# Index queries first, closings by column halves, and background work in finer steps, in a two-layer encoder on one core

## The chip, the core and the metric

The kernel runs as one program on one core of a Trainium2 chip. The engines have each their own instruction stream: PE multiplies matrices (and PEld loads its stationary operand), DVE and ACT do elementwise work, POOL a little of it, SP issues most transfers. The metric is the device time of one execution in microseconds (us).

## The reference

Two layers, each a mixer and a gated feed-forward network (FFN) with a convolution, on 512 positions of 1024 channels, in float32. Layer norm follows each of the two, with the residual scaled by ALPHA.

```python
for l in range(DEPTH):                                   # 2
    y = hybrid_mixer(x, positions, w_in[l], ..., w_out[l], b_out[l])
    x = layer_norm(DN_ALPHA * x + y, ln1_g[l], ln1_b[l])
    y = conv_ffn(x, w_up[l], conv_w[l], conv_b[l], w_down[l])
    x = layer_norm(DN_ALPHA * x + y, ln2_g[l], ln2_b[l])
...
# hybrid_mixer: proj = x @ w_in, split into aq, ak, av, iq, ik, iw, gq, gk, gv, g_lr, g_r, gate_a, gate_b
ya = dsa_attention(aq, ak, av, iq, ik, iw) @ p_attn      # iq.ik scores choose 128 keys a query; softmax over these
log_a = log_sigmoid(g_lr @ gla_w_gate + gla_b_gate) / 16
o = gla_chunked(gq, gk, gv, log_a)                       # state = exp(total) * state + k_dec^T v, by chunks of 64
yb = (norm(o) * silu(g_r)) @ p_gla
return (sigmoid(gate_a) * ya + sigmoid(gate_b) * yb) @ w_out + b_out
...
# conv_ffn: u = causal_conv3(x @ w_up) + conv_b; a, b = split(u); return (gelu(a) * b) @ w_down
```

## The kernel before

Every large product is made of three: each float32 operand is split into a rounded high part (ACT, line 144) and the rest (DVE, line 145), and `mm3` issues high x low, low x high and high x high (lines 149 to 151). A weight tile of 128 x 1024 (512 KB) is loaded by SP into one of three raw buffers (line 130) and split into one of five; `weight` keeps four tiles ahead, in the fixed order of `plan_all`. The split of a weight has priority in the schedule.

The input lies transposed in `xT` (8 tiles of 128 channels x 512 positions, high and low). `tm_chunk` makes a projection with positions in partitions: four quarters g of two weight rows each, and for every quarter the four position blocks tb; `fm_tile` makes one with channels in partitions. Sums are held in banks: `acc` has four, `tps` (transposes, and the state updates of the scans) and `sps` two each.

What isn't a projection runs as tasks. A task is a generator; `tick`, called every six products or so, lets each task issue its next step, up to its next `yield`. So the number of yields says how many products of the projections stand between two steps of a task. The tile framework then schedules all this into one fixed order for each engine.

Layer 0 begins with 14 warm-up products (line 905), the constants, the small projections (`do_small`: the index key, its weights and the decay's input, in a bank of `acc`), and the index queries "iq". During "gk", `decay_task` makes the decay logits (line 373), takes logarithms, splits them block by block and sums them by a triangular matrix (L390). `index_task` transposes the roped queries (L447, evacuated by `stack`), scores them (L476) and takes the largest 128 by rounds of max and match_replace (L509, L510). Two `scan_task`s, for two heads each, run beside the value, attention query and key projections: `update` (L536) makes both half-block contributions, DVE adds them to the state (L545, the first is copied, L542), the state is split, and `read` multiplies the queries with it.

`closing` is the last product of a mixer (`wout`) and of an FFN (`wdB`, eight of its 22 rows). It works by halves of the positions: two blocks x two column halves in four banks, and for both halves of the positions every weight row (128 x 1024) is loaded and split again. Its last three rows (five at the very end) are done sum by sum; DVE adds each sum to x (L837), and `norm` follows at once: statistics (L716, L718), an inverse root (`rstd`, a POOL operation L292 within, and L291 to L296 on DVE), two passes over x (L722, L723), and the transposes of x (L729) into `xT`, with their splits.

Of the kernel before, what the change touches and what calls it, by code (L numbers as in the profile page):

```python
# [23 lines left out]
RANK = 16  # L24
# [31 lines left out]
class Trunk:  # L56
# [86 lines left out]
    def split(self, hi, lo, src):  # L143
        self.nc.scalar.copy(hi, src)  # L144
        self.nc.vector.tensor_sub(lo, src, hi.bitcast(F32))  # L145

# [18 lines left out]
    def tm_chunk(self, l, chunk, evac, pairs=((0, 1, 2, 3),), between=None):  # L165
        ws = []
        for pair in pairs:
# [3 lines left out]
            for g in range(4):  # L171
                if len(ws) <= g:
                    ws.append(self.weight((l, chunk, g)))
                w = ws[g].rearrange("p z (k n) -> p z k n", k=2)
                for j, tb in enumerate(pair):
                    for kk in range(2):
                        k = 2 * g + kk
                        c = slice(tb * 128, (tb + 1) * 128)
                        self.mm3(ps[j], self.xT[:, k, 0, c], self.xT[:, k, 1, c], w[:, 0, kk], w[:, 1, kk],
                                 k == 0, k == KT - 1)  # L180
# [13 lines left out]
    def constants(self):  # L194
# [21 lines left out]
        self.xT = c.tile([128, KT, 2, S], F32R, name="xT")  # L216

    def rope_tables(self):
# [3 lines left out]
        nc.scalar.dma_start(pi_, self.a["positions"])  # L222
# [43 lines left out]
    def layer_consts(self, l):  # L266
# [3 lines left out]
        for r in (0, 32, 64):  # L270
            nc.scalar.dma_start(raw[r:r + RANK + 1, :], a["w_gate"][l])
# [4 lines left out]
        nc.scalar.dma_start(self.normg, a["norm_g"][l])  # L276
        self.convw = self.lay.tile([128, 2 * NF, 3], F32, name=self.name("cw"), tag="cw")
        nc.scalar.dma_start(self.convw, a["conv_w"][l])
        self.convb = self.lay.tile([128, 2 * NF], F32, name=self.name("cb"), tag="cb")
        nc.scalar.dma_start(self.convb, a["conv_b"][l])  # L280
# [19 lines left out]
    def plan_all(self, l):  # L300
# [38 lines left out]
        for half in range(2):  # L339
            for k in range(KA, NF):  # L340
                P((l, "wdB", half, k), (a["w_down"][l, k * 128:(k + 1) * 128, :], None))
# [4 lines left out]
    def do_small(self, l):  # L346
        nc = self.nc
        w = self.weight((l, "small")).rearrange("p z (k m) -> p z k m", k=KT)
        ps = self.bank(self.acc)
# [12 lines left out]
    def decay_task(self):  # L362
# [22 lines left out]
        for tb in range(TB):  # L385
            lt = self.u()
            self.split(lt[:, 0], lt[:, 1], mn[tb // 2][:, tb % 2])
            e = self.bank(self.sps)
# [53 lines left out]
    def transpose_task(self, src, dst, keep):  # L442

        for hp in range(4):
# [4 lines left out]
            dst.append(keep(ps))  # L449
            yield  # L450
# [65 lines left out]
    def scan_task(self, h0, deps):  # L516
# [8 lines left out]
        state = self.h().rearrange("p (h v) -> p h v", h=2)  # L525
        halves = (slice(0, 64), slice(64, 128))

        def update(tb):
# [9 lines left out]
            for j, o in enumerate(kv):  # L538
                c = 2 * tb + j
                with self.tc.high_priority():  # L540
                    if c == 0:
                        nc.vector.tensor_copy(state, o)  # L542
                    else:
                        for i, h in enumerate(hs):
                            nc.vector.scalar_tensor_tensor(state[:, i], state[:, i], self.dec[:, h, c:c + 1], o[:, i],  # L545
                                                           op0=ALU.mult, op1=ALU.add)
                    t = self.u(F32R, (128, 2, 2, DV))
                    self.split(t[:, 0], t[:, 1], state)
# [161 lines left out]
    def norm(self, tb, g, b, last=False):  # L710
# [9 lines left out]
        for j in range(2):  # L720
# [3 lines left out]
            if last:  # L724
                nc.sync.dma_start(self.out[tb * 128:(tb + 1) * 128, c], x[:, c])
                continue
# [5 lines left out]
            self.split(xt[:, :, 0], xt[:, :, 1], ps.rearrange("p (k t) -> p k t", k=4))  # L732


    def mixer(self, l):
# [73 lines left out]
        self.closing(l, "wout", self.merged, 0, KT, lambda tb: self.norm(tb, g, b))  # L809

    def closing(self, l, key, src, k0, k1, norm):

        nc = self.nc
        for half in range(2):
            late = 5 if k0 and l == L - 1 and half else 3
            tbs = (2 * half, 2 * half + 1)
            ps = {(tb, n): self.bank(self.acc) for tb in tbs for n in range(2)}
            ws = {}

            def mm(tb, n, k):  # L820
                c, f = slice(tb * 128, (tb + 1) * 128), slice(n * 512, (n + 1) * 512)
                w = ws[k]
                self.mm3(ps[tb, n], src[k][:, 0, c], src[k][:, 1, c], w[:, 0, f], w[:, 1, f], k == k0, k == k1 - 1)
            for k in range(k0, k1 - late):
                ws[k] = self.weight((l, key, half, k))
                for tb in tbs:
                    for n in range(2):
                        mm(tb, n, k)
                self.tick()
            for k in range(k1 - late, k1):  # L830
                ws[k] = self.weight((l, key, half, k))
            for tb in tbs:
                for n in range(2):
                    f = slice(n * 512, (n + 1) * 512)
                    for k in range(k1 - late, k1):
# [123 lines left out]
```

## Time and profile before

| | |
|---|---|
| median of 3 runs | 1817.56 us (1816.87 to 1820.11) |
| the profiled execution | 1819.35 us, its span 1817.6 us |
| PE busy | 1783.6 us, 98% of the span |
| DVE / ACT busy | 1182.3 us (65%) / 789.4 us (43%) |
| moved by DMA | 186.17 MB, mean 102 GB/s |

All times in the rows are from the profiled execution, in us from the start of its span. Matmuls are pipelined: a row shows some 0.39 us for one of 512 columns, while the next starts earlier, so the pace is read from starts. Idle time of an engine matters only if PE, in the end, waits for it.

### The profile page before, as it was taken

Reading aid. Unit: us, or ns where it says so; the run is one execution under the profiler, and the core shown is the slowest. Engines: PE = TensorE matmul, PEld = TensorE weight load, DVE = VectorE, ACT = ScalarE, POOL = GpSimd, SP = SyncE. Lnnn points to the kernel's source line nnn. Section 1 sums busy time; section 2 is a strip of 40 time slices with the busy share of each in tenths; the row PEclk is TensorE's granted clock in tenths of the full one; section 3 lists DMA queues with packets and bytes.
Section 4 is the critical chain, followed back from the end, with each engine's and each line's share of the span. In section 5 each row is a group of like instructions: output and inputs, shape, how many; then the busy total and the mean of one; then the engine's idle time right before and its main releaser. Section 6 shows DMA issues by size and latency. Waiting matters only on the chain.

```text
span 1817.6 us, 21860 instructions
## 1 busy us (share of the span) xinstructions
PE 1783.6 (98%) x8286; PEld 1430.7 (79%) x8286; DVE 1182.3 (65%) x2205; ACT 789.4 (43%) x1187; POOL 35.5 (2%) x57
## 2 busy tenths in 40 slices
PE   8999999999999999999999999999999999999997
PEld 6777777888888888888777777778888888888885
DVE  6899768733496553356768996786335865632567
ACT  5744566622334442244356346674223354421441
POOL 0000000000000000000000000000000000000000
PEclk9999999999999999999999999999999999999999
DMA  5221231232453222322631223312325332223334
GB/s 193 64 74 66 70 105 58 70 105 89 142 198 95 95 99 94 93 93 93 211 127 59 70 70 88 87 59 70 105 93 193 131 116 93 93 93 94 95 112 140
DMA packets 57350, 186.17 MB, mean 102 GB/s; under 512 B 6711, under 2 KB 6967, under 8 KB 57245
## 3 DMA queue, kind: packets, MB, share of 16 engines
q1 hardware_dynamic: 51680, 170.74, 29.4%
q10 hardware_dynamic: 4284, 11.94, 1.9%
q0 software_dynamic: 1280, 2.10, 0.5%
q8 instruction: 65, 1.06, 0.3%
q14 instruction: 41, 0.33, 0.1%
HBM read 178.46 MB, written 4.19 MB: 100 GB/s over the span
## 4 chain that ended last, share of the span: by engine, by line
PE 80%; DVE 8%; issue 4%; DMA 4%; ACT 3%; POOL 1%; ACTq 0%; POOLq 0%; DVEq 0%; SPq 0%
PE ps L149 25%; PE ps L151 24%; PE ps L150 24%; DVE w L145 2%; DMA raw<-in_w_down 1%; PE ps L476 1%; PE ps L477 1%; ACT w L144 1%; PE ps L622 1%; POOL rs L292 1%; DMA raw<-in_w_mix_out 1%; DVE sc L510 1%; PE ps L632 0%; PE ps L447 0%; PE ps L729 0%
## 5 line engine op out<-in xcount | busy, mean ns | idle before, releaser
L145 DVE TENSOR_TENSOR w<-raw,w 128x1024 fp32r<-128x1024 f32 (+1 forms) x320 | 387.2, 1215 | 488.4 <-ACT w L144 487.7
L144 ACT CAST w<-raw 128x1024 fp32r<-128x1024 f32 (+1 forms) x320 | 332.1, 1043 | 522.0 <-PE ps L151 422.7
L149 PE MATMUL ps<-xT,w 128*128 128x512 f32 (+2 forms) x1232 | 476.7, 387 | 1.3 <-DVE xT L145 1.3
L151 PE MATMUL ps<-xT,w 128*128 128x512 f32 (+2 forms) x1232 | 473.1, 384 | 0.0
L150 PE MATMUL ps<-xT,w 128*128 128x512 f32 (+2 forms) x1232 | 473.1, 384 | 0.0
L149 PEld LDWEIGHTS ps<-xT,w 128*128 128x128 f32 (+1 forms) x1232 | 231.4, 188 | 49.7 <-DVE xT L145 2.8
L151 PEld LDWEIGHTS ps<-xT,w 128*128 128x128 f32 (+1 forms) x1232 | 231.2, 188 | 49.2
L150 PEld LDWEIGHTS ps<-xT,w 128*128 128x128 f32 (+1 forms) x1232 | 231.4, 188 | 45.8
L149 PE MATMUL ps<-w,u 128*128 128x512 f32 x480 | 190.5, 397 | 5.2 <-DVE u L837 2.6
L150 PE MATMUL ps<-w,u 128*128 128x512 f32 x480 | 189.6, 395 | 0.0
L151 PE MATMUL ps<-w,u 128*128 128x512 f32 x480 | 189.3, 396 | 0.0
L149 PE MATMUL ps<-w,xT 128*128 128x512 f32 x448 | 180.9, 404 | 2.8 <-DVE w L145 1.8
L151 PE MATMUL ps<-w,xT 128*128 128x512 f32 x448 | 177.9, 397 | 0.0
L150 PE MATMUL ps<-w,xT 128*128 128x512 f32 x448 | 177.8, 397 | 0.0
L144 ACT CAST u<-h 128x512 fp32r<-128x512 f32 x108 | 66.7, 620 | 199.5 <-DVE h L858 108.6
L149 PEld LDWEIGHTS ps<-w,u 128*128 128x128 f32 x480 | 90.4, 188 | 29.8 <-DVE u L837 4.3
L151 PEld LDWEIGHTS ps<-w,u 128*128 128x128 f32 x480 | 90.4, 188 | 20.8
L150 PEld LDWEIGHTS ps<-w,u 128*128 128x128 f32 x480 | 90.4, 188 | 20.3
L149 PEld LDWEIGHTS ps<-w,xT 128*128 128x128 f32 x448 | 84.6, 189 | 22.7 <-DVE w L145 2.3
L151 PEld LDWEIGHTS ps<-w,xT 128*128 128x128 f32 x448 | 84.3, 188 | 19.8
L145 DVE TENSOR_TENSOR u<-h,u 128x512 fp32r<-128x512 f32 x108 | 74.0, 688 | 38.1 <-ACT u L144 37.8
L150 PEld LDWEIGHTS ps<-w,xT 128*128 128x128 f32 x448 | 84.4, 188 | 17.1
(200 smaller groups left out, 2070.3 us busy)
## 6 DMA issues: line engine op xcount, KB each, us to landing
raw<-in_w_fm SPq DMA_DIRECT2D x160, 512.0 KB, 3.5
raw<-in_w_down SPq DMA_DIRECT2D x60, 512.0 KB, 3.5
raw<-in_w_tm SPq DMA_DIRECT2D x56, 512.0 KB, 3.6
raw<-in_w_mix_out SPq DMA_DIRECT2D x32, 512.0 KB, 4.1
raw<-in_p_attn SPq DMA_DIRECT2D x8, 512.0 KB, 3.3
u<-in_xT SPq DMA_DIRECT2D x8, 256.0 KB, 4.7
u<-u POOLq DMA_DIRECT2D x16, 128.0 KB, 3.0
u<-in_x ACTq DMA_DIRECT2D x4, 512.0 KB, 4.9
```

Of the source, the lines that this page charges most:

```text
L144: self.nc.scalar.copy(hi, src)
L145: self.nc.vector.tensor_sub(lo, src, hi.bitcast(F32))
L149: mm(out, lh, rl, start=start, stop=False)
L150: mm(out, ll, rh, start=False, stop=False)
L151: mm(out, lh, rh, start=False, stop=stop)
L292: self.nc.gpsimd.tensor_tensor(r, ve, self.nhalf[:, :n], ALU.pow)
L476: mm(out, q, k, start=True, stop=False)
L477: mm(out, q, kl, start=False, stop=True)
L510: nc.vector.match_replace(sc, m8, sc, TAKEN)
L622: nc.tensor.transpose(ps[:, qb * 128:(qb + 1) * 128], P[qb][:, sb * 128:(sb + 1) * 128], self.ident)
```

## The change

- Layer 0: the small projections come behind the index queries, in a bank of `sps`; the first index weights and the first two xT tiles are loaded in turn (two half-tile loads of weights), then a weight tile for every two tiles of xT; six of 14 warm-up products go; constants, rope tables and the small loads on ACT's queue are issued behind the loading of xT. The first quarter is walked row by row (`k_outer`).
- Tasks: the decay's splits are made one block ahead, with two more yields; a transposing task yields twice for each bank; the scan's read yields once more; the scan has two state buffers, and its first state is split directly from the bank.
- Closings: by column halves. The first half walks the weights with four blocks in four banks; the second half keeps its four weight tiles and does one block after the other. A weight tile is two rows x 512 columns, and each is loaded once: 8 tiles a closing, not 16. The norm is a task: it issues its arithmetic at once and its transposes some ticks later; the FFN and the next layer finish the tasks before they use a block.

```diff
@@ tm_chunk
+                if k_outer:
+                    for j, tb in enumerate(pair):
+                        mm(j, tb, 0)
                 for j, tb in enumerate(pair):
...
+                    for kk in range(k_outer, 2):
+                        mm(j, tb, kk)
@@ plan_all
-        if l == 0:
-            small()
         for g in range(4):
             P((l, "iq", g), (a["w_tm"][l, TM_CHUNKS.index("iq"), g], None))
-        if l:
-            small()
+        small()
...
-        for half in range(2):
-            for k in range(KT):
-                P((l, "wout", half, k), (a["w_mix_out"][l, k * 128:(k + 1) * 128, :], None))
+        for n in range(2):
+            for k in range(0, KT, 2):
+                P((l, "wout", n, k), rows(a["w_mix_out"], k, n))
@@ decay_task
-        for tb in range(TB):
-            lt = self.u()
-            self.split(lt[:, 0], lt[:, 1], mn[tb // 2][:, tb % 2])
+        ahead = parts(0)
+        yield
+        yield
+        for tb in range(TB):
+            lt = ahead
+            if tb < TB - 1:
+                ahead = parts(tb + 1)
@@ transpose_task
             dst.append(keep(ps))
             yield
+            yield
@@ scan_task, update and the loop
+                    t = self.u(F32R, (128, 2, 2, DV))
                     if c == 0:
-                        nc.vector.tensor_copy(state, o)
+                        self.split(t[:, 0], t[:, 1], o)
+                        nc.vector.tensor_copy(states[1], o)
                     else:
+                        old, state = states[c % 2], states[1 - c % 2]
...
             for j in range(2):
+                yield
                 yield
                 read(tb, j, ss[j])
@@ norm -> norm_task(self, tb, g, b, last, wait)
+        if last:
+            return
+        for _ in range(wait):
+            yield
+        for j in range(2):
             ps = self.bank(self.tps)
...
+            yield
@@ mixer
-            self.do_small(l)
-            self.tm_chunk(l, "iq", self.roped(iq))
+            self.tm_chunk(l, "iq", self.roped(iq), k_outer=True)
+            self.do_small(l, self.sps)
         else:
-            self.tm_chunk(l, "iq", self.roped(iq), [(0, 1), (2, 3)], lambda: self.do_small(l))
+            self.finish(*self.norms[:2])
+
+            def between():
+                self.finish(*self.norms)
+                self.do_small(l, self.acc)
+            self.tm_chunk(l, "iq", self.roped(iq), [(0, 1), (2, 3)], between)
@@ closing (new body)
+        self.norms = []
+        ps = [self.bank(self.acc) for _ in range(TB)]
+        for k in range(k0, k1, 2):
+            w = self.weight((l, key, 0, k))
+            for tb in range(TB):
+                mm(ps[tb], tb, k, w)
+                self.tick()
+                if k == k1 - 2:
+                    add(ps[tb], tb, 0)
+        ws = {}
+        for tb in range(TB):
+            ps = self.bank(self.acc if tb > 1 else self.sps)
+            for k in range(k0, k1, 2):
+                if not tb:
+                    ws[k] = self.weight((l, key, 1, k))
+                mm(ps, tb, k, ws[k])
+                self.tick()
+            add(ps, tb, 1)
+            self.norms.append(self.spawn(norm(tb)))
+            self.step(self.norms[-1])
@@ ffn
         for tok in ((0, 256), (256, 512)):
+            self.finish(*self.norms[tok[0] // 128:tok[1] // 128])
@@ run
-        for _ in range(14):
+        for _ in range(8):
...
+            for k in range(2):
+                c = slice(512 * k, 512 * k + 512)
+                nc.sync.dma_start(raws[0][:, k], self.a["xT"][k])
+                nc.sync.dma_start(raw[:, c], src[0][:, c])
+                self.split(self.xT[:, k, 0], self.xT[:, k, 1], raws[0][:, k])
+                self.split(w[:, 0, c], w[:, 1, c], raw[:, c])
...
+        self.constants()
+        self.rope_tables(last)
```

Where the instructions now stand. First PE at the program's start, before; `w_133` is the small projections' weight, `ps_234` their bank.

```order
L905 MATMUL ps_90<-u_87 128x512 x14
L149 MATMUL ps_234<-xT,w_133 104x512
L150 MATMUL ps_234<-xT,w_133 104x512
L151 MATMUL ps_234<-xT,w_133 104x512
L149 MATMUL ps_234<-xT,w_133 104x512
```

The same place after the change; `w_105` is the first index weight tile, `ps_227` to `ps_230` the banks of the four position blocks (lines are those of the changed file, L150 to L152 being `mm3`).

```order
L941 MATMUL ps_89<-u_87 128x512 x8
L150 MATMUL ps_227<-w_105,xT 128x512
L150 MATMUL ps_228<-w_105,xT 128x512
L150 MATMUL ps_229<-w_105,xT 128x512
L150 MATMUL ps_230<-w_105,xT 128x512
L151 MATMUL ps_227<-w_105,xT 128x512
```

The products with the low part of the weight now come first, for all four blocks, ahead of the first that needs the low part of xT.

Second, DVE at the start of layer 0's second scan, before; `ps_1580` is the first contribution, `u_1595` the low part of the split state, `sc` and `m` belong to the top-k rounds.

```order
L542 COPY h_1579<-ps_1580 128x512
L510 MATCH_REPLACE sc_757<-m_1542,sc_757 128x384
L509 MAX m_1554<-sc_757 128x8
L145 TENSOR_TENSOR u_1595<-h_1579,u_1595 128x512
L510 MATCH_REPLACE sc_757<-m_1554,sc_757 128x384
L545 SCALAR_TENSOR_TENSOR h_1579<-h_1579,dec_443,ps_1581 128x256 x2
```

The same place after; `ps_1574` is the contribution, `u_1588` the low part.

```order
L145 TENSOR_TENSOR u_1588<-ps_1574,u_1588 128x512
L559 COPY h_1573<-ps_1574 128x512
L300 TENSOR_TENSOR rs_1543<-rs_1543,rs_1541 128x8
L525 MATCH_REPLACE sc_784<-m_1612,sc_784 128x384
L563 SCALAR_TENSOR_TENSOR h_1572<-h_1573,dec_436,ps_1575 128x256 x2
```

The split has moved ahead of the copy, and the top-k operations that stood between the two follow.

Third, DVE in the mixer closing of layer 0, before: from the second pass over block 0 (`u_4254`) to that over block 1 (`u_4256`); each L145 with `w` is a weight split.

```order
L723 SCALAR_TENSOR_TENSOR u_4254<-u_4254,rs_4400,u_4264 128x512 x2
L145 TENSOR_TENSOR w_4518<-raw_4516,w_4518 128x1024
L145 TENSOR_TENSOR w_4535<-raw_4533,w_4535 128x1024
L145 TENSOR_TENSOR xT<-ps_4410,xT 128x4x128
L145 TENSOR_TENSOR w_4552<-raw_4550,w_4552 128x1024
L145 TENSOR_TENSOR xT<-ps_4419,xT 128x4x128
L291 TENSOR_SCALAR rs_4451<-mv_4449 128x1
L722 SCALAR_TENSOR_TENSOR u_4256<-u_4256,mv_4449,u_4262 128x512
L293 TENSOR_TENSOR rs_4453<-rs_4452 128x1
L722 SCALAR_TENSOR_TENSOR u_4256<-u_4256,mv_4449,u_4262 128x512
L145 TENSOR_TENSOR w_4569<-raw_4567,w_4569 128x1024
```

The same stretch after; blocks 0 and 1 are `u_4249` and `u_4251`.

```order
L741 SCALAR_TENSOR_TENSOR u_4249<-u_4249,rs_4441,u_4259 128x512 x2
L853 TENSOR_TENSOR u_4251<-ps_4453,u_4251 128x512
L734 BN_STATS bs_4486<-u_4251 128x6
L145 TENSOR_TENSOR xT<-ps_4478,xT 128x4x128
L736 BN_AGGR mv_4489<-bs_4486 128x2
L297 TENSOR_SCALAR rs_4491<-mv_4489 128x1
L740 SCALAR_TENSOR_TENSOR u_4251<-u_4251,mv_4489,u_4257 128x512
L299 TENSOR_TENSOR rs_4493<-rs_4492 128x1
L740 SCALAR_TENSOR_TENSOR u_4251<-u_4251,mv_4489,u_4257 128x512
L300 TENSOR_TENSOR rs_4493<-rs_4493,rs_4491 128x1
L145 TENSOR_TENSOR xT<-ps_4511,xT 128x4x128
L301 TENSOR_SCALAR rs_4493<-rs_4493 128x1
```

The four weight splits have left this stretch, and the addition and statistics of the next block have entered it.

## Rows read from the trace of the kernel before

**Rows 1.** The page's list of engines: busy us, share of the span, instructions.

```profile
PE 1783.6 (98%) x8286; PEld 1430.7 (79%) x8286; DVE 1182.3 (65%) x2205; ACT 789.4 (43%) x1187; POOL 35.5 (2%) x57
```

**Rows 2.** Timeline of PE, index queries: start, us, engine, line, operation.

```profile
36.70 0.39 PE L149 MATMUL ps<-w,xT 128*128 128x512 f32 x1
...
41.37 0.40 PE L151 MATMUL ps<-w,xT 128*128 128x512 f32 x1
```

**Rows 3.** Waits of PE: who waited for whom, us in total, times, longest.

```profile
PE ps L149 <- DVE u L145: 3.8, 4, 1.8
PE ps L390 <- DVE u L145: 3.0, 2, 1.5
PE ps L149 <- DVE u L837: 2.6, 3, 1.0
PE ps L447 <- DVE u L458: 2.4, 2, 1.2
PE ps L149 <- DVE rs L295: 2.2, 2, 2.0
PE ps L149 <- DVE w L145: 2.2, 2, 1.8
...
PE ps L729 <- DVE u L723: 1.6, 3, 0.8
```

**Rows 4.** Timeline of PE, the program's start; in brackets the wait ahead.

```profile
2.06 5.00 PE L905 MATMUL ps<-u 128*128 128x512 f32 x14 [2.06 <-DVE u L901]
...
7.72 0.48 PE L149 MATMUL ps<-xT,w 128*104 128x512 f32 x1 [0.67 <-DVE xT L145]
...
16.41 0.50 PE L149 MATMUL ps<-w,xT 128*128 128x512 f32 x1 [1.81 <-DVE w L145]
...
22.37 0.50 PE L149 MATMUL ps<-w,xT 128*128 128x512 f32 x1 [1.03 <-DVE u L359]
...
41.61 0.52 PE L409 MATMUL ps<-ident,h 104*128 104x104 f32 x4
```

**Rows 5.** Timeline of PE, the decay sums of layer 0.

```profile
60.12 0.73 PE L390 MATMUL ps<-u,tri 128*128 128x512 f32 x2 [1.49 <-DVE u L145]
```

**Rows 6.** Timeline of PE, second scan; and a window behind it (PE busy, PEclk granted).

```profile
167.97 0.36 PE L149 MATMUL ps<-u,u 128*128 128x256 f32 x1 [1.78 <-DVE u L145]
...
169.00:173.00 4.00, 4.00 (x14) 0.57 0.00 0
```

**Rows 7.** Windows of 20 us: length, then PE, PEld, DVE, ACT, POOL busy.

```profile
100.00:120.00 20.00, 20.00 (x97) 15.95 (x96) 19.61 (x40) 6.79 (x10) 0.00 (x0) 1.00 0.29 87
...
200.00:220.00 20.00, 18.73 (x86) 14.59 (x86) 12.70 (x32) 12.04 (x20) 1.65 (x1) 1.00 0.25 79
```

**Rows 8.** Timeline of PE, mixer closing of layer 1.

```profile
1415.77 0.50 PE L149 MATMUL ps<-w,u 128*128 128x512 f32 x1 [2.01 <-DVE rs L295]
```

**Rows 9.** Timeline of ACT, first casts; and a window (the last column is GB/s).

```profile
4.29 0.63 ACT L144 CAST w<-raw 128x104 fp32r<-128x104 f32 x2 [0.59 <-DMA raw<-in_w_small]
...
4.98 0.62 ACT L144 CAST xT<-u 128x512 fp32r<-128x512 f32 x1
...
4.00:6.00 2.00, 2.00 (x8) 1.59 (x7) 1.32 (x8) 1.65 (x5) 0.00 (x0) 1.00 1.01 348
```

**Rows 10.** The page's costliest groups: busy us, mean ns; idle before, releaser.

```profile
L145 DVE TENSOR_TENSOR w<-raw,w 128x1024 fp32r<-128x1024 f32 (+1 forms) x320 | 387.2, 1215 | 488.4 <-ACT w L144 487.7
L144 ACT CAST w<-raw 128x1024 fp32r<-128x1024 f32 (+1 forms) x320 | 332.1, 1043 | 522.0 <-PE ps L151 422.7
```

**Rows 11.** Timeline of DVE, the last block's norm.

```profile
1808.61 0.69 DVE L837 TENSOR_TENSOR u<-ps,u 128x512 f32<-128x512 f32 x1 [0.30 <-PE ps L151]
...
1812.86 1.41 DVE L723 SCALAR_TENSOR_TENSOR u<-u,rs,u 128x512 f32<-128x512 f32 x2
```

**Rows 12.** The warm-up line alone: duration ns, min/median/max.

```profile
L905 PE MATMUL ps<-u x14: 387/546/796, 2.1 to 6.7; 128*128 128x512 f32 x14
```

**Rows 13.** Timeline of DVE, beside the scans.

```profile
155.36 0.17 DVE L293 TENSOR_TENSOR rs<-rs 128x8 f32<-128x8 f32 x1 [1.26 <-POOL rs L292]
```

More of the change, by code (lines that the diff above doesn't have):

```diff
@@ L143, in split @@
     def split(self, hi, lo, src):
-        self.nc.scalar.copy(hi, src)
+        first = self.nc.scalar.copy(hi, src)
         self.nc.vector.tensor_sub(lo, src, hi.bitcast(F32))
+        return first
     def mm3(self, out, lh, ll, rh, rl, start, stop):
@@ L163, in fm_tile, with tm_chunk @@
         return ps
-    def tm_chunk(self, l, chunk, evac, pairs=((0, 1, 2, 3),), between=None):
+    def tm_chunk(self, l, chunk, evac, pairs=((0, 1, 2, 3),), between=None, k_outer=False):
         ws = []
@@ L215, in constants, with rope_tables @@
         nc.gpsimd.memset(self.bias0[0:64, 64:128], NEG)
-        self.xT = c.tile([128, KT, 2, S], F32R, name="xT")
-    def rope_tables(self):
+    def rope_tables(self, prev):
         nc, c = self.nc, self.cst
@@ L338, in plan_all, with do_small @@
             fm(FM["up"] + m)
-        for half in range(2):
-            for k in range(KA, NF):
-                P((l, "wdB", half, k), (a["w_down"][l, k * 128:(k + 1) * 128, :], None))
+        for n in range(2):
+            for k in range(KA, NF, 2):
+                P((l, "wdB", n, k), rows(a["w_down"], k, n))
     order = ["gk", "gq0", "gq1", "gv0", "gq2", "gq3", "gv1", "aq", "ak", "av"]
-    def do_small(self, l):
+    def do_small(self, l, pool):
         nc = self.nc
         w = self.weight((l, "small")).rearrange("p z (k m) -> p z k m", k=KT)
-        ps = self.bank(self.acc)
+        ps = self.bank(pool)
         for k in range(KT):
@@ L524, in scan_task @@
         mv = self.small([128, TB, 2, 2], tag="mv")
-        state = self.h().rearrange("p (h v) -> p h v", h=2)
+        states = [self.h().rearrange("p (h v) -> p h v", h=2) for _ in range(2)]
         halves = (slice(0, 64), slice(64, 128))
@@ L708, with norm_task @@
     MERGE = ["a0", "a1", "b0", "a2", "b1", "a3", "b2", "a4", "b3", "a5", "b4", "a6", "b5", "a7", "b6", "b7"]
-    def norm(self, tb, g, b, last=False):
+    def norm_task(self, tb, g, b, last, wait):
         nc = self.nc
@@ L808, in mixer @@
             nc.vector.scalar_tensor_tensor(self.x[tb], self.x[tb], ALPHA, bo, op0=ALU.mult, op1=ALU.add)
-        self.closing(l, "wout", self.merged, 0, KT, lambda tb: self.norm(tb, g, b))
+        self.closing(l, "wout", self.merged, 0, KT, lambda tb: self.norm_task(tb, g, b, False, 4 if tb < 3 else 8))
     def closing(self, l, key, src, k0, k1, norm):
         nc = self.nc
[L814 to L828, printed above, removed]
-                self.tick()
[L830 to L835, printed above, removed]
-                        mm(tb, n, k)
-                    nc.vector.tensor_add(self.x[tb][:, f], ps[tb, n], self.x[tb][:, f])
-                norm(tb)
@@ new lines, in mm, with add @@
+        def mm(ps, tb, k, w):
+            c = slice(tb * 128, (tb + 1) * 128)
+            w = w.rearrange("p z (k n) -> p z k n", k=2)
+            for kk in range(2):
+                self.mm3(ps, src[k + kk][:, 0, c], src[k + kk][:, 1, c], w[:, 0, kk], w[:, 1, kk], k + kk == k0,
+                         k + kk == k1 - 1)
+        def add(ps, tb, n):
+            f = slice(n * 512, (n + 1) * 512)
+            nc.vector.tensor_add(self.x[tb][:, f], ps, self.x[tb][:, f])
+        self.norms = []
@@ L891, in ffn @@
         g, b = self.row("ln2_g", l), self.row("ln2_b", l)
-        self.closing(l, "wdB", gT, KA, NF, lambda tb: self.norm(tb, g, b, last=l == L - 1))
+        self.closing(l, "wdB", gT, KA, NF, lambda tb: self.norm_task(tb, g, b, l == L - 1, 4))
         if l < L - 1:
```

59 lines of the change are left out of this document (34 added, 25 removed).

## The prediction

> **What bounds the kernel now.** I read the page's list of engines first: PE is busy 98% of the span [rows 1], so time can only come from the moments in which PE stands, or from fewer or faster products; the change leaves every product in place but six of the fourteen warm-up ones. A steady run shows the pace: 21 products of 512 columns start between 36.70 and 41.37 us, so one per 4.67 / 20 = 0.2335 us [rows 2]. Next I read who PE waited for. Every long entry names DVE, and none names a weight transfer [rows 3]: the lower half of a split (L145), the input of the decay sums (L390), the addition that empties a sum (L837), the transposes (L447, L729), the norm (L295). Then I went to each place in the timeline.
>
> The head: the first product starts at 7.72 us, and six products of the first "gk" quarter are done at 41.61 us [rows 4]. That stretch holds 24 products for the small projections, 96 for the index queries and those six: 126 x 0.2335 = 29.4 us of work in 33.9 us. The 4.5 us between are mostly two waits, 1.81 us for the first index weights and 1.03 us until the small projections' bank is read out [rows 4].
>
> The gk stretch: PE stands 1.49 us at L390 for the split of the decay logarithms [rows 5]; layer 1 repeats it, together 3.0 us in the list [rows 3].
>
> The scans: PE stands 1.78 us for the split of a scan's first state [rows 6]. Right behind it the granted clock falls: over the four microseconds shown its mean is 0.57, so for most of them PE ran at the lower of its two levels, 1.2 GHz, and lost some 4 x 0.43 = 1.7 us of work. Layer 1 has the wait again, without the fall (the list has 3.8 us for these and two small ones [rows 3]). DVE is 19.6 of 20 us busy ahead of it, and only 12.7 of 20 once the scans are over [rows 7]: here DVE is as scarce as PE.
>
> The closings: the lines L837, L723 and L295 of the list plus 0.4 us of the w line and 0.3 us elsewhere, 2.6 + 1.6 + 2.2 + 0.7 = 7.1 us over four closings [rows 3]; the longest single one is 2.01 us, for a block's norm [rows 8].
>
> **The change part by part.** *The head.* The first index product needs one xT tile and half a weight tile, 512 KB. Before, 672 KB (416 KB small weights, one xT tile) had landed when the cast at 4.98 us began, and the 416 KB when the casts at 4.29 us began [rows 9]. DMA moves some 350 GB/s there [rows 9], 0.75 us per 256 KB, so 512 KB land by about 4.5 us; the cast takes 0.62 us [rows 9] and the weight's lower half lies beside it, so PE starts at about 5.25 us: 2.45 us earlier. Does it run dry behind that? Each index quarter brings 1 MB, 3.0 us of transfer, for 24 products of 5.6 us, and DVE needs 1.2 us for the weight tile [rows 10] and twice some 0.7 for xT (a 512-column operation [rows 11]), under 3 us of these 5.6. So the 4.5 us of waits go; I leave 0.3 of them. What is late next: the small projections now end directly ahead of gk, so the copy of their sums (behind one 1.04 us weight cast on ACT [rows 10], since that buffer is freed by the same products), the index keys' transposes and the four decay logits follow PE by only 2 to 5 us. By the rows' durations I find about 0.25 us at the keys' transposes, 0.5 at the third logit (two banks, each emptied by DVE between a dozen rope operations) and 0.4 at the second transposes: 1.2 us (bounds 0 and 3). Head: -2.45 - 4.2 + 1.2 = -5.45 us. The moved constants and rope tables cost nothing: their 25 or so small operations come while PE has index products for 22 us, and the sine is wanted at the first roped query, some 23 us in. The two quarter-size weight loads are covered as shown.
>
> *Fewer warm-ups.* The fourteen start at 2.06 us [rows 4] and took from 387 to 796 ns each, median 546 [rows 12], where a product at full pace shows 390 to 400 [rows 2]: the first of them ran slower. With eight, from about 1.6 us, they end near 5.1 us. The page "TensorE: Matmul & The Clock Gate" of the Trainium skill (Part 1) says that the clock is throttled by default, that activity releases it, and that the number of cold products changes from run to run; by it the first index products could still run at half pace. For the sum I bound it by rows: nothing if the eight do what the fourteen did, or the loss of the scans' fall once more, 1.7 us [rows 6]. I take 0, since eight from 1.6 us on still fill more than 3 us, and keep 1.7 as the other end.
>
> *Decay.* Splitting one step ahead and two more steps give the chain from the logits some 2.8 us more. Two waits of 1.49 us go, but in layer 0 the chain starts later, as told; with 0.3 us left each: -2.4 us (bounds 0 and -3.0).
>
> *Scans.* The first state is split directly from its bank, so a copy of some 0.7 us and two top-k operations leave DVE's row ahead of the split, and the read is issued behind 24 products of the projections, not 12: 12 x 0.2335 = 2.8 us more against a wait of 1.78. It goes in both layers, with the fall of the clock: -3.5 - 1.7 - 0.2 = -5.4 us (bounds -1.5 and -5.5). The second state buffer costs nothing while the six half-size buffers turn: the key projection's copies come after the second scan's last update. What is late next: the longer scan of the second head pair now lies beside the transposes of the attention queries, and both want the two transpose banks.
>
> *Transposes.* Of the 2.4 us at L447 [rows 3] I give back half for that reason: -1.2 us (bounds 0 and -2.4).
>
> *Closings.* By halves of columns, 32 weight tiles of 64 go, each 1.04 us of ACT and 1.22 of DVE [rows 10]; no wait for them was on PE's list except 0.4 us, so that alone gives little. What counts is the norm. From the addition to the first finished half is 1808.61 to 1812.86 plus half of 1.41: 4.95 us [rows 11]; to the second half 5.66. The transposes of a block now stand behind 24 products, 5.6 us. So block 0 arrives in time by about 0.3 us. Block 1 starts 0.3 us late, and two xT splits of 0.69 stand in its chain: it misses by about 1 us. In layer 0 to 1 and in the two mixer closings something like 1 to 1.8 us stays at that place or at the first product that needs the last transposes; I take 1.2 us for each of three closings, and none for the last, which has no transposes: 3.6 against 7.1, -3.5 (bounds +2 and -7). The tail behind the last product is the same chain; block 2's chain of 5.66 us now has 5.6 us of products over it, so the last addition is up to 0.3 us later: +0.3.
>
> **Sum.** -5.45 - 2.4 - 5.4 - 1.2 - 3.5 + 0.3 = -17.65 us. The profiled execution took 1819.35 us (its span 1817.6 and 1.75 around it), so 1801.7 us; it stands 1.8 us above the median of the runs, 1817.56, and the forecast for the median is 1799.9 us.
>
> **Rivals.** *A: only the head counts.* DVE is 98% busy in the scans, so what PE doesn't wait for at one place it waits for at the next, and the closings' waits move to the first users of xT. For it: [rows 7]. Against it: DVE has 7 us free in the stretch behind [rows 7], and its work for the scans falls by no product of PE. Then -5.45 and perhaps 1 us more: 1811 us.
>
> *B: slower, by the norms in the closings.* In the second half DVE has four chains of 5.66, eight xT splits of 0.69 and five weight splits of 1.22, together 34.3 us, over 96 products of 22.4 us. The overhang of 12 us is harmless as long as the next products don't need the last two blocks: the FFN opens with 96 half-width products (about 11.2 us, half of 0.2335 each), and layer 1 with 48 full ones (11.2 us). If the overhang falls on PE instead, from the point at which that cover is used up, each of three closings loses up to 12 us; with all three lost, 1799.9 + 3.5 + 36 = 1839 us, and with half of it 1821. DVE does stand behind a waiting instruction: at 155.36 us it had waited 1.26 us for POOL [rows 13], in a stretch in which it had other work queued. The same page of the skill says in Part 1 (engine queue depths) that VectorE and ScalarE work strictly in order; this trace agrees by that wait. Against it: the chains also hold 1 us waits for POOL that the splits can fill.
>
> *C: everything goes.* All bounds at their good end: -6.65 - 3 - 5.5 - 2.4 - 7 = -24.6, 1793 us.
>
> **How the numbers follow.** The forecast's own range is 1794 to 1806 us, chance 0.62. A (1806 to 1814) has 0.20, C with all below 1794 0.08, B 0.05, and a cancelling within 0.2%, the early end of B, 0.05. About 0.2%, 3.6 us, is what a measurement of this kernel can tell from no change. To hold 8 in 10 the range takes in most of A: 1793.5 to 1811. Faster by over 0.2% (under 1813.9) is the forecast, C and nearly all of A: 0.90; within 0.2% 0.05, slower by more 0.05.
>
> **What would show it.** First index product near 5.3 us, gk's first six done near 35.5, no wait over 0.5 us at L404 and no clock under 1.00 in the first scans; about 1 us before the second block's transposes in each of the first three closings; the last addition at most 0.3 us behind the last product's former distance. It is wrong if PE's list after shows waits of several us for xT at the opening of the FFN or of layer 1 (B), or if the split of a state still ends waits of over 1 us (A).

## The result and the profile after

The changed kernel took 1799.0 us (median of 4 runs, 1798.15 to 1800.04) where the kernel before took 1818.1 beside it: a ratio of 0.9894, 95% interval [0.9877, 0.9911], so 19 us less. The forecast was 1799.9. The total was right; several of the parts below it were not, as the experiments show. The profiled execution took 1798.15 us, its span 1796.4.

The page's list of engines after, which answers to [rows 1]:

```profile
PE 1770.9 (99%) x8280; PEld 1436.5 (80%) x8280; DVE 1150.0 (64%) x2172; ACT 758.4 (42%) x1154; POOL 35.6 (2%) x57
```

DVE and ACT have lost 32 and 31 us; the 32 weight tiles that the closings no longer load twice account for it (1215 and 1043 ns each in [rows 10], so 38.9 and 33.4 us). PE lost 12.7 us of its busy time.

Who PE waited for in the kernel after (us in total, times, longest), against [rows 3]:

```profile
PE ps L150 <- DVE u L145: 2.9, 2, 1.5
PE ps L461 <- DVE h L270: 2.4, 5, 0.7
PE ps L404 <- DVE u L145: 2.3, 3, 1.2
PE ps L751 <- DVE u L741: 2.2, 4, 0.7
...
PE ps L150 <- DVE sh L592: 1.4, 2, 0.7
PE ps L461 <- ACT h L445: 1.4, 2, 0.7
```

The entries of the closings (L837, L295, and "w" of the head) are gone. What is left stands at four places: the scans' reads (L150 behind u or sh, 4.3 us), the transposes of attention operands (L461, 3.8), the decay sums (L404, 2.3), the norms' transposes (L751, 2.2).

The head in the timeline of PE after (start, us, engine, line, operation), and below it the first "gk" product before:

```profile
1.53 3.78 PE L941 MATMUL ps<-u 128*128 128x512 f32 x8 [1.53 <-DVE u L938]
5.10 1.50 PE L150 MATMUL ps<-w,xT 128*128 128x512 f32 x4
6.44 0.39 PE L151 MATMUL ps<-w,xT 128*128 128x512 f32 x1
...
33.52 0.39 PE L150 MATMUL ps<-w,xT 128*128 128x512 f32 x1
...
34.90 0.40 PE L150 MATMUL ps<-w,xT 128*128 128x512 f32 x1
...
35.40 0.55 PE L423 MATMUL ps<-ident,h 104*128 104x104 f32 x4
```

```profile
40.20 0.40 PE L149 MATMUL ps<-w,xT 128*128 128x512 f32 x1
```

The first index product starts at 5.10 us and gk at 33.52, where it started at 40.20 before: 6.7 us earlier. Its seventh product starts at 34.90, where [rows 4] has 41.61 behind the first six. The index keys' transposes at 35.40 (L423) now stand behind eight products of gk: 33.52 + 8 x 0.2335 = 35.39, so no wait is left there.

The second scan in the same view: its first update and its first three reads. Then a window ahead of the third read (length, busy PE, PEld, DVE, ACT, POOL, granted clock, DMA share, GB/s):

```profile
154.40 0.97 PE L551 MATMUL ps<-u,u 64*128 64x256 f32 x12
...
159.58 0.28 PE L150 MATMUL ps<-u,u 128*128 128x256 f32 x1
...
163.98 0.35 PE L150 MATMUL ps<-u,u 128*128 128x256 f32 x1 [0.73 <-DVE sh L592]
...
173.05 0.39 PE L150 MATMUL ps<-u,u 128*128 128x256 f32 x1 [1.43 <-DVE u L145]
```

```profile
169.00:173.00 4.00, 2.62 (x12) 1.79 (x10) 3.96 (x10) 1.74 (x3) 0.00 (x0) 1.00 0.04 2
```

The first read (159.58) no longer waits, as [rows 6] did for 1.78 us; the two behind it wait 2.16 us together. Between the update and the first read stand 18 products of the projections; in the kernel before there were 12. In the window the clock is at its upper level, and DVE is 3.96 of 4 us busy.

Behind the scans, the transposes of the attention keys in PE's timeline, and ACT's timeline there:

```profile
214.41 0.49 PE L461 MATMUL ps<-ident,h 128*128 128x128 f32 x2
215.59 0.30 PE L461 MATMUL ps<-ident,h 128*128 128x128 f32 x1 [0.69 <-ACT h L445]
216.58 0.30 PE L461 MATMUL ps<-ident,h 128*128 128x128 f32 x1 [0.69 <-DVE h L270]
```

```profile
211.96 1.09 ACT L597 ACTIVATE u<-u,sh,rs 128x256 f32<-128x256 f32 x2
212.96 0.57 ACT L445 COPY h<-ps 128x512 f32<-128x512 f32 x1
213.42 0.61 ACT L597 ACTIVATE u<-u,sh,rs 128x256 f32<-128x256 f32 x1
213.93 0.57 ACT L445 COPY h<-ps 128x512 f32<-128x512 f32 x1
214.40 0.61 ACT L597 ACTIVATE u<-u,sh,rs 128x256 f32<-128x256 f32 x1
214.90 0.57 ACT L445 COPY h<-ps 128x512 f32<-128x512 f32 x1
```

The key copies (L445), for which the transposes wait, stand between the normalising activations of the second scan (L597): that scan now ends just when the keys come out. In the kernel before, its last normalising activation ended at 215.00 and the first key copy began at 219.32.

The norms' transposes behind two closings, in PE's timeline, against [rows 8]; and the last block's norm in DVE's, against [rows 11]:

```profile
515.75 0.60 PE L751 MATMUL ps<-ident,u 128*128 128x128 f32 x4
...
526.96 0.63 PE L751 MATMUL ps<-ident,u 128*128 128x128 f32 x4 [0.40 <-DVE u L741]
...
532.97 0.63 PE L751 MATMUL ps<-ident,u 128*128 128x128 f32 x4 [0.64 <-DVE u L741]
...
1419.52 0.63 PE L751 MATMUL ps<-ident,u 128*128 128x128 f32 x4 [0.47 <-DVE u L741]
...
1425.54 0.63 PE L751 MATMUL ps<-ident,u 128*128 128x128 f32 x4 [0.68 <-DVE u L741]
```

```profile
1786.80 0.68 DVE L853 TENSOR_TENSOR u<-ps,u 128x512 f32<-128x512 f32 x1
...
1791.05 1.41 DVE L741 SCALAR_TENSOR_TENSOR u<-u,rs,u 128x512 f32<-128x512 f32 x2
```

In both mixer closings the first two blocks come in time: the second block's transposes (515.75) have no wait. It is the third and the fourth block that miss, by 0.40 and 0.64 us in layer 0 and by 0.47 and 0.68 in layer 1, and these transposes already stand among the first products of the FFN. The closing between the layers has one such wait, of 0.18 us. The last chain is as long as before, 1786.80 to 1791.05 against 1808.61 to 1812.86; the span ends 9.6 us behind the last addition, before 9.0.

### The profile page after: what moved, and what is told of

Same layout as the page of the kernel before. It is cut to its first block, busy times and chain, and to the rows that moved or that the text cites. A ratio compares the mean times of both kernels' runs of the same rounds, so it can differ in the third digit from the quotient of the medians.

```text
span 1796.4 us, 21646 instructions
## 1 busy us (share of the span) xinstructions
PE 1770.9 (99%) x8280; PEld 1436.5 (80%) x8280; DVE 1150.0 (64%) x2172; ACT 758.4 (42%) x1154; POOL 35.6 (2%) x57
## 4 chain that ended last, share of the span: by engine, by line
PE 60%; DVE 5%; issue 3%; ACT 1%; POOL 1%; POOLq 0%; DVEq 0%; ACTq 0%
PE ps L152 19%; PE ps L150 19%; PE ps L151 19%; DVE w L145 1%; DVE u L741 1%; POOL rs L298 1%; PE ps L491 1%; PE ps L492 1%; PE ps L640 0%; DVE u L740 0%; DVE sc L525 0%; DVE bs L734 0%; DVE xT L145 0%; DVE u L853 0%; DVE u L145 0%
## 5 line engine op out<-in xcount | busy, mean ns | idle before, releaser
L145 DVE TENSOR_TENSOR w<-raw,w 128x1024 fp32r<-128x1024 f32 (+2 forms) x287 | 349.6, 1218 | 488.9 <-ACT w L144 488.2
L144 ACT CAST w<-raw 128x1024 fp32r<-128x1024 f32 (+2 forms) x287 | 299.8, 1045 | 482.9 <-PE ps L152 415.8
L150 PE MATMUL ps<-xT,w 128*128 128x512 f32 (+2 forms) x1232 | 475.4, 386 | 0.0
L152 PE MATMUL ps<-xT,w 128*128 128x512 f32 (+2 forms) x1232 | 472.6, 384 | 0.0
L152 PEld LDWEIGHTS ps<-xT,w 128*128 128x128 f32 (+1 forms) x1232 | 231.7, 188 | 48.1
L150 PEld LDWEIGHTS ps<-xT,w 128*128 128x128 f32 (+1 forms) x1232 | 231.9, 188 | 45.9
L150 PE MATMUL ps<-w,u 128*128 128x512 f32 x480 | 190.3, 397 | 0.0
L152 PE MATMUL ps<-w,u 128*128 128x512 f32 x480 | 189.4, 395 | 0.0
L150 PE MATMUL ps<-w,xT 128*128 128x512 f32 x448 | 179.7, 402 | 0.0
L152 PE MATMUL ps<-w,xT 128*128 128x512 f32 x448 | 177.9, 397 | 0.0
L150 PEld LDWEIGHTS ps<-w,u 128*128 128x128 f32 x480 | 90.4, 188 | 21.1 <-issue 0.3
L152 PEld LDWEIGHTS ps<-w,u 128*128 128x128 f32 x480 | 90.4, 188 | 21.0
L152 PEld LDWEIGHTS ps<-w,xT 128*128 128x128 f32 x448 | 84.3, 188 | 19.3
L150 PEld LDWEIGHTS ps<-w,xT 128*128 128x128 f32 x448 | 85.0, 190 | 18.0 <-DVE w L145 0.3
L145 DVE TENSOR_TENSOR u<-h,u 128x512 fp32r<-128x512 f32 x104 | 71.3, 689 | 38.7 <-ACT u L144 38.4
```

The costliest lines, as they stand in the source:

```text
L144: first = self.nc.scalar.copy(hi, src)
L150: mm(out, lh, rl, start=start, stop=False)
L152: mm(out, lh, rh, start=False, stop=stop)
```

## The experiments

All were timed beside the kernel before, whose medians were 1817.5 to 1818.6; so a difference of some 1 us between two rows is not resolved. The waits are those of PE's list in each trace (us): reads of the scans, transposes of attention and index operands, decay sums, norms' transposes (blank where the closings are still those of the kernel before).

| kernel | us | ratio to before, 95% | reads | transposes | decay | norms |
|---|---|---|---|---|---|---|
| after | 1799.0 | 0.9894 [0.9877, 0.9911] | 4.3 | 3.8 | 2.3 | 2.4 |
| e1 head | 1809.7 | 0.9958 [0.9944, 0.9972] | 3.3 | 2.6 | 2.6 | |
| e2 closings | 1810.1 | 0.9960 [0.9947, 0.9972] | 3.8 | 2.8 | 3.0 | 2.3 |
| e3 finer steps | 1813.7 | 0.9983 [0.9974, 0.9992] | 3.8 | 3.5 | 2.3 | |
| e4 head, closings | 1800.3 | 0.9904 [0.9891, 0.9918] | 3.5 | 2.6 | 2.5 | 2.3 |
| e5 transposes at once | 1803.0 | 0.9914 [0.9899, 0.9929] | 4.3 | 3.8 | 2.3 | 3.9 |
| e6 after, old scans | 1795.8 | 0.9876 [0.9859, 0.9893] | 4.0 | 0.3 | 2.3 | 2.5 |
| e7 after, one step | 1804.5 | 0.9921 [0.9908, 0.9934] | 4.4 | 7.3 | 2.1 | 3.4 |
| e8 shifted | 1795.6 | 0.9876 [0.9861, 0.9890] | 4.4 | 4.3 | 0.8 | 1.6 |
| e9 after, no extra step | 1795.6 | 0.9879 [0.9865, 0.9892] | 3.2 | 2.7 | 2.3 | 2.4 |
| e10 POOL splits | 1809.7 | 0.9953 [0.9940, 0.9965] | 7.9 | 3.1 | 2.0 | 2.4 |
| e11 14 warm-ups | 1800.1 | 0.9905 [0.9889, 0.9920] | 4.3 | 3.6 | 2.3 | 2.8 |
| e12 ends spread | 1792.5 | 0.9860 [0.9844, 0.9877] | 3.2 | 0.6 | 2.3 | 2.4 |

The intervals are wide because the runs of before spread, by up to 8.3 us (1814.16 to 1822.41); the runs of one experiment spread by 0.7 (e6: 1795.64 to 1796.29) to 4.2 us (e3).

**Which part carries the gain: e1 to e4.** The parts of the diff put on the kernel before, one by one, and the first two together:

```
e1: small() behind the index weights; tm_chunk(..., k_outer=True); do_small(l, self.sps) behind it;
    new loading order in run(); range(14) -> range(8) warm-ups; loads of constants behind `last`
e2: plan_all, closing, norm_task, finish(*self.norms...) of after
e3: decay_task, transpose_task, scan_task of after
e4: e1 and e2
```

> The kernel before with the head alone (index queries first, their loading order, the small projections behind them, eight warm-up products). Theory (head and closings carry the gain, the finer steps little): 6 to 7 us less than before, about 1811.5, since gk started 6.7 us earlier in the trace of after. Rival (the prediction's own sum): 5.45 less, about 1812.7. If the head only counts because the finer steps follow it: under 4 us less.

> The kernel before with the closings alone (column halves, two k rows per tile, norm as a task). Theory: about 9 us less than before, 1809 (the closings' stalls of 8.9 us on products go, the tail costs 0.6). Rival (the prediction's sum): 3.2 less, 1815.

> The kernel before with the finer steps alone (decay split one step ahead, one more step behind each transposed quarter, two states and one more step ahead of a read). Theory: waits move to later reads and transposes, so only some 1.5 to 3.5 us less than before, about 1815.5 (the decay's half and the clock's fall of 1.7). Rival (the prediction's sum): 2.4 + 5.4 + 1.2 = 9 us less, 1809.

> The kernel after without the finer steps (head and closings alone on the kernel before). Theory: 15 to 16.5 us less than before, about 1802.5, so within 4 us of the kernel after. Rival (the prediction's sum): 8.65 less, 1809.4, 10 us behind the kernel after.

Measured: -7.8, -7.4, -3.8 and -17.2 us against the median beside them. Head and closings bring nine tenths of the 19 us; the finer steps bring 3.8 alone (3.1 by the ratio) and between 1 and 2 on top of the others. The theory holds in kind, though e1, e3 and e4 gained more than it said (6 to 7, 1.5 to 3.5 and 15 to 16.5) and e2 less (9); the prediction's own split (5.45, 3.2, 9.0) falls, since by it e4 would be 1809.

e2 settles another point. Its second scan waits as in the kernel before, but the clock stays up. PE's timeline and the window behind:

```profile
167.53 0.36 PE L149 MATMUL ps<-u,u 128*128 128x256 f32 x1 [1.77 <-DVE u L145]
```

```profile
168.00:172.00 4.00, 4.00 (x24) 3.11 (x23) 3.93 (x11) 2.59 (x4) 0.00 (x0) 1.00 0.03 13
```

So the fall of [rows 6] is no fixed price of that wait. The trace of before shows the same: layer 1 has the wait again (1.72 us at 1068.89), and the granted clock over 1069 to 1073 us is 1.00. It comes and goes: beside e1 to e4 the mean clock of the 15 runs of before lay between 0.997 and 0.999, and e3, whose first read doesn't wait, still had 0.997 in three of 11.

**Do the closings need the steps that are written down: e5.**

```diff
-        for _ in range(wait):
+        for _ in range(0):
             yield
```

> The kernel after, the norms' transposes issued at once behind each norm and not four or eight steps later. Theory (what the closings gain is that a block's norm has one block's 24 products, 5.6 us, over it; the number of steps written down matters little where the order places the transposes some 20 products behind anyway): 0 to 3 us more than after, 1799 to 1802, with longer waits at L751. Rival (the steps make the closings' gain): the gain of the closings alone, 7.4 us, goes back, about 1806.

4.0 us more than after, a little over the theory's 3 and far from the rival's 7.4. In the trace the first block's transposes wait 0.57 us at 509.55, where they waited for nothing, and the list's entry grows:

```profile
PE ps L751 <- DVE u L741: 3.6, 9, 0.6
```

About half of the closings' gain hangs on the steps. The rest is put down to the halves of columns, with which a block's norm has the next block's products over it; this is not shown, as the halves of columns have no run of their own.

**The finer steps one by one: e6, e7, e9.**

```diff
e6: scan_task of the kernel before in the kernel after
e7: transpose_task
             dst.append(keep(ps))
-            yield
             yield
e9: scan_task
             for j in range(2):
-                yield
                 yield
                 read(tb, j, ss[j])
```

> The kernel after with the scans as in the kernel before (one state, first state copied before it is split, a read one step earlier). Theory (waits only move from the first read to later ones): within 1.5 us of the kernel after, about 1799.5, with the 1.8 us wait at the first read of the second scan back and the two later ones gone. Rival (the prediction): 5.4 us more, 1804.4; without the clock's fall 3.7 more, 1802.7.

> The kernel after with one step, not two, behind each transposed quarter. Theory: the waits of the transposes move from the rotated rows back to the banks, 3.8 us of them become some 2.5: between 1 us less and 1 us more than after. Rival (the prediction): 1.2 us more; if the second step does harm: over 1 us less, 1798 or under.

> The kernel after without the extra step ahead of a scan's read, its two states and the direct split of the first state kept. With the whole scan change undone the time was 1795.8, 3.2 less than after. Theory (the extra step makes the second scan end some 8 steps later, so that its normalising on ACT and its updates on DVE fall on the rotated rows that the attention's transposes wait for): the transposes' 3.8 us of waits go as in that run, and the first read of the second scan no longer waits 1.7, so 1793 to 1796. Rival (the two states or the direct split do the harm, by a buffer or by DVE's order): about 1799, the waits at L461 still over 3 us.

e6 was 3.2 us faster than after, which neither theory had: the scan change does harm. e7 was 5.5 us slower: the second step behind a transposed quarter is worth far more than predicted. e9 gives the whole 3.2 us back while it keeps the two states and the direct split, so the harm lies in the extra step ahead of a read. (Its waits are spread otherwise than in e6: the first read's 1.70 us fell to 0.63, with 0.79 at the second, but 2.1 us stand at the transposes behind the banks.) PE's waits in e6:

```profile
PE ps L150 <- DVE u L145: 4.0, 6, 1.7
...
PE ps L461 <- DVE u L473: 0.3, 2, 0.2
```

The reads wait as long as in after, 4.0 against 4.3, but the transposes 0.3 against 3.8. What moved stands in ACT's timeline of e9:

```profile
196.64 4.05 ACT L596 ACTIVATE u<-u,sh,rs 128x256 f32<-128x256 f32 x8 [1.14 <-DVE sh L591]
...
209.11 0.59 ACT L445 COPY h<-ps 128x512 f32<-128x512 f32 x1 [0.34 <-PE ps L152]
```

Without the extra step the second scan's normalising starts at 196.64 and is done 8 us before the first key copy. With it, it starts at 208.43 and stands among the copies. The second scan's first update starts at nearly the same time in both (153.73 and 154.40); eight steps more, of six products each, are 48 x 0.2335 = 11.2 us, and they moved its end by 12 us into the one place where ACT and DVE are waited for. In e7 both effects meet: the queue of quarters fills the two banks (2.6 us behind the stacks, L472) and still stands behind the rotated rows:

```profile
PE ps L461 <- DVE h L270: 4.2, 7, 0.9
...
PE ps L461 <- DVE u L472: 2.6, 4, 1.2
```

**Warm-ups: e11.** `range(8)` becomes `range(14)`.

> The kernel after with fourteen warm-up products, not eight. Theory (as in the prediction, fewer cost nothing): within 1 us of after, 1798 to 1800; the six more products of about 0.4 us end later than the first tiles arrive, so up to 1.5 us more is possible. Rival (the first products run at a lower pace for want of warm-ups): up to 1.7 us less, 1797.3, with the first four index products at 0.24 us each.

1.1 us more than after, with ranges that overlap (1799.61 to 1801.01, after 1798.15 to 1800.04). In the traces the first product starts at 7.23 instead of 5.10, 2.1 us later, but at full pace, and the index keys' transposes 1.6 us later (36.98 against 35.40). With eight, the first four products (row at 5.10) take 6.44 - 5.10 = 1.34 us, 0.4 more than at 0.2335 each. That is one execution: in the traces of the ten kernels that have the new head with eight warm-ups these four took from 0.95 (e7) to 1.70 us (e10). So the low pace that the prediction bounded by 1.7 us cost 0.0 to 0.8.

**Is DVE's load the limit: e10, on the kernel of e6.**

```diff
+                if key[1] in ("gk", "gv0", "gv1", "aq") and key[2] % 2:
+                    self.nc.scalar.copy(w[:, 0], raw)
+                    self.nc.gpsimd.tensor_sub(w[:, 1], raw, w[:, 0].bitcast(F32))
```

> The kernel after with the whole scan change undone, and every second weight tile of gk, gv0, gv1 and aq gets its lower half on POOL, which is idle, not on DVE (8 of them per layer, 9.8 us of DVE). Theory (the waits left at the scans' reads, 4.0 us, are DVE's backlog): 2 to 3 us less than 1795.8, about 1793. Rival (POOL is slower at such a subtraction and the weight comes late, or slows DVE beside it): 1796 to 1805, with waits of PE for a weight tile from POOL.

The rival's side, and past its end: 13.8 us more than e6. Sixteen subtractions left DVE, yet the reads wait 7.9 us and two projections 2.6 more, all behind DVE; no wait of PE is for a weight tile from POOL. POOL takes twice DVE's 1.21 us (e10's groups of POOL). In DVE's timeline seven operations, each beside another of the sixteen subtractions, last until POOL's subtraction ends. The first fence has POOL, with the subtraction of 151.44 to 153.84; the second has four of the seven, which take 0.19, 0.29, 0.41 and 0.15 us elsewhere:

```profile
L135 POOL TENSOR_TENSOR w<-raw,w 128x1024 fp32r<-128x1024 f32 x16 | 38.8, 2423 | 226.9 <-ACT w L134 191.2 <-DVE u L477 25.0 <-DMA cb<-in_conv_b 8.8
...
151.44 2.40 POOL L135 TENSOR_TENSOR w<-raw,w 128x1024 fp32r<-128x1024 f32 x1 [0.97 <-POOL rs L302]
```

```profile
21.87 2.36 DVE L249 SCALAR_TENSOR_TENSOR h<-h,h 128x32 f32<-128x32 f32 x1
...
33.22 2.32 DVE L270 TENSOR_TENSOR ra<-h,cos 128x128 f32<-128x128 f32 x1
...
78.19 2.14 DVE L518 TENSOR_SCALAR sc<-r,iw 128x384 f32<-128x384 f32 x1
...
151.71 2.16 DVE L305 TENSOR_SCALAR rs<-rs 128x8 f32<-128x8 f32 x1
```

The other three lie in layer 1 (1.67, 2.13 and 2.18 us). Together the seven lasted 13.0 us more than the same operations in e6, against some 19 us that the sixteen subtractions took on DVE; each ended at most 0.21 us behind POOL's subtraction. The Trainium skill, "SBUF — State Buffer" (section "SBUF: two separate sides"), says that a VectorE operation in a 2-port mode, or one with two SBUF inputs against a GpSimd operation that reads SBUF, and the GpSimd operation lock a shared port against each other for the whole instruction. The seven agree with that: three have two inputs from SBUF, and four are TENSOR_SCALAR operations, whose mode no trace shows. Other operations beside POOL kept their length (0.70 us for a MAX8 of 512 columns). How much of the reads' waits comes from this stays open; the order in which DVE's work stands changed too.

**Faster versions: e8 and e12.**

```diff
e8 (on after): three yields ahead of the attention's transposes; top-k pauses while a second-scan
    update waits for its first read; one more yield in decay_task; wait 4 -> 5
e12 (on e9): three yields ahead of the attention's transposes, and
-        r = self.rstd(...)            # POOL's power and DVE's Newton step in one go
-        ... eight activations
+        self.spawn(self.scan_end(hs, on, mv))   # power; two yields; Newton; a yield, two activations, ...
```

> A try at a faster version: the kernel after, and in it the attention's transposes start three steps behind their projection, the top-k steps pause while an update of the second scan waits for its first read, the decay's sums stand one more step behind the splits, and the transposes of a norm five steps behind, not four. Theory (PE waits there only because DVE works off other things first): of 3.8 us at the transposes 3 go, of 4.3 at the scans' reads 3, of 2.3 at the decay 1.5, of 2.4 at the norms' transposes 1: about 8 less than after, 1791. Rival (DVE is full, a wait taken away here comes back at the next place): within 2 us of after, 1798 to 1801.

> A try at the fastest version: the kernel after without the extra step ahead of a scan's read (1795.6 by itself), the end of a scan (POOL's power, the Newton step, eight normalising activations) as a task of its own over several steps so that DVE doesn't stand behind POOL in the next scan, and the attention's transposes three steps behind their projection. Theory (the waits left at the transposes, 2.7 us, and part of the reads' 3.2 are work that is in the way for no need): 1.5 to 3.5 us less, 1792 to 1794. Rival (DVE's total work sets these stretches, so a wait moves): 1795 to 1797.

e8 gained 3.4 of 8 us. The reads still wait 4.4 us, but the pause was no test: from 164.86 to 170.73 us DVE still runs six rounds of top-k in a row ahead of the second block's update, as in the kernel after, so whether they hold the reads stays open. The norms' later transposes cost 1.9 us at the first users of xT, and what the decay's sums gained came back at the index transposes (0.95 us at 51.37). e12 is the fastest kernel, 1792.5 us, 6.5 less than after and within its forecast. Its list of waits:

```profile
PE ps L150 <- DVE u L145: 3.2, 6, 0.8
PE ps L404 <- DVE u L145: 2.3, 3, 1.2
PE ps L764 <- DVE u L754: 2.2, 4, 0.7
...
PE ps L463 <- DVE u L475: 0.6, 2, 0.3
```

Against e9 the transposes' waits fell from 2.7 to 0.6 us and nothing else moved in the list: 2.1 of the 3.1 us. Which of its two edits did that was not run apart.

## Why the prediction was right, and where it was wrong

- *Head, -5.45:* -7.8 by e1. The start (5.10 against 5.25) came as worked out. So did the waits: 33.52 - 5.10 = 28.4 us for 120 products of 0.2335, 28.0, and the 0.4 left is the low pace of the first four. The term that failed is the 1.2 us of new waits behind the small projections; they did not come. In e1 gk starts 6.6 us earlier (33.56 against 40.20), and its first eight products run at pace up to the keys' transposes (8 x 0.2335 = 1.87):

```profile
33.56 0.39 PE L150 MATMUL ps<-w,xT 128*128 128x512 f32 x1
...
35.43 0.55 PE L412 MATMUL ps<-ident,h 104*128 104x104 f32 x4
```

  The rest of the difference, about 1 us, is no larger than the spread of the runs.
- *Warm-ups, 0:* right in size, as the bound of 1.7 was too wide: 0.0 to 0.8 us at the first products, and with fourteen the kernel is 1.1 slower. The reason given for the 0, the time that eight products fill, rests on no row; behind the same eight the first products were slow in some executions and not in others.
- *Decay, -2.4:* 3.0 us of waits became 2.3. Between the split and the sums stands DVE's queue, which two steps don't outlast. Wrong by its size; no run has it alone.
- *Scans, -5.4:* wrong in sign beside the other parts. The step read "the read is issued behind 24 products of the projections, not 12" and looked at the first read alone. One step more brought 18, so 6 x 0.2335 = 1.4 us and not 2.8. The first read's wait went all the same, but a wait came at the next two; the clock's fall, 1.7 us of the term, is no fixed price of that wait; and the extra step's other effect, a later end of the second scan, cost 3.2 us (e6, e9). The prediction had named the place ("the longer scan of the second head pair now lies beside the transposes") and the wrong resource: banks instead of ACT's and DVE's queues.
- *Transposes, -1.2:* -5.5 by e7, beside the extra scan step, or -4.5 by e4 against e6, which has the new decay besides. It was discounted by half for a cost that belongs to the scans.
- *Closings, -3.5 and +0.3:* -7.4 by e2. The step that failed is the chain of the second block, which was to miss by 1.2 us in three closings; it missed in none. Left behind were 2.3 us and not 3.6, at the third and the fourth block. The larger error is on the other side: 7.1 us, the sum of the list, was too little. By the starts of PE's products, e2 gains 0.6, 3.8, 1.6 and 2.2 us on the kernel before in the four closings, 8.1 together, where the list gives 7.1 - 2.3 = 4.8. The list leaves out waits under 0.15 us and counts the others short: its 1.01 us at 1789.49 in the last closing before is 1.18 by the starts. The tail costs 0.6 and not 0.3. The last addition comes as close behind the last product as before; the 0.6 lies behind the chain of the last norm, and no run shows why.
- *Rivals:* A's mechanism (a wait comes back at the next place) is right for the scans' reads, and wrong for the total. The prediction's own sign for A, a split of a state that still ends waits of over 1 us, did come (1.43 at 173.05, and 1.45 in layer 1). B is excluded: no wait of several us at the opening of the FFN or of layer 1. What should show each step showed the head right. The closings showed no wait at the second block, where about 1 us was expected; against the decay stands a wait over 0.5 us at L404 (0.92 at 52.53), and there are waits at L461.

So two errors cancelled: head and closings gave 6.5 us more than forecast (8.6 by e4), the finer steps 5 to 8 less. That the total came within 1 us of the forecast is luck.

## What to carry to other kernels

A step that delays one consumer also delays everything behind it in the same task: look at where the task's end lands, and whom it meets there. When a wait is to go, ask what the next user of the same engine does in that moment, and undo each part of a change by itself, since parts that were meant to help can cost what others bring.

## What the hardware showed that was not expected

The clock's fall behind a wait is not a property of the place: the same wait of 1.78 and 1.77 us at the same read went with a clock of 0.57 in the trace of before and of 1.00 in that of e2. The pace of the first products behind the same eight warm-ups differed too, 0.95 to 1.70 us for four, while the granted clock of after reads 1.00 from 5.00 to 6.50 us, where its four took 1.34. The Trainium skill, "TensorE: Matmul & The Clock Gate" (Part 1), says that the number of cold products differs from run to run. The spread of these ten traces agrees with that; that the clock is the cause is not shown, as its record reads 1.00. And POOL's subtraction of 128x1024 took 2.42 us, twice DVE's, and seven of sixteen held an operation of DVE, one of them of 0.15 us for 2.16 us.
